# RWKV units: state decay and two products on GpSimd, the group norm's scaling and k's factor on ScalarE, one running sum per head pair

## The chip, the cores and the metric

The kernel runs on one core of a Trainium2 chip. The metric is the device time of one execution in microseconds. A core has five instruction queues that run beside each other, each in its own order, tied by semaphores: PE (TensorE, matmuls, with its weight loads listed as PEld), DVE (VectorE), ACT (ScalarE), POOL (GpSimd) and SP (SyncE, which here mostly issues DMA transfers).

## The reference

One layer of a hybrid decoder for a prompt of 1024 tokens and a group of 8 single tokens, in float32. One projection of the normalized input feeds three branches: RWKV-7 time mixing with 8 heads of 64, sliding-window attention, and cross-attention. They are merged with sigmoid gates, and a squared-ReLU MLP follows. The change lies in the RWKV branch alone:

```python
w_log = -softplus(-(w0 + tanh(wd) @ w2)) - 0.5
decay = exp(-exp(w_log));  a = sigmoid(a0 + ad @ a2);  g = sigmoid(gd) @ g2
kk = heads(k * k_k);  kk = kk / max(norm(kk), 1e-12)
kh = heads(k * (1 + (a - 1) * k_a))
# per head and token:
sa = S @ -kk_t
S  = S * decay_t + outer(sa, kk_t * a_t) + outer(v_t, kh_t)
y  = S @ r_t
# then a group norm over each head's 64 values:
y  = (y - mean(y)) * rsqrt(var(y) + 64e-5) * ln_w + ln_b
out = (y + sum(r * kh * r_k) * v) * g
```

## The kernel before

All 1032 tokens are held as columns, channels on partitions. A dense float32 product is made of three matmuls, since both sides are split into a high and a low part (`dense`, L181 to L183). `in_proj` (L254) makes 128 output columns of the input projection: 72 matmuls on weights of 512 KB; ScalarE casts the high part of the weights (L173), GpSimd subtracts it for the low part (L174).

The RWKV branch runs in chunks of 64 tokens. `unit(jj, q)` (L428) handles two pairs of heads and a quarter of the prompt, 256 tokens; a tile of 128 x 512 holds both pairs. There are eight units, the last of each jj with the 8 single tokens added. A unit is a generator in three parts:

- Preparation, to the first yield: loads of r, k, v (tiles zr, zk, zv); decay logarithm lw and a (tile aa) from two small products; running sums of lw within each chunk (L468); the norm of kk; k's factor (L490, L491); the products r·k (L494, L496) whose sums go through DRAM (`bsum`) and return spread over partitions as rn and bv; exponentials of the sums (L529, L530); and the two operands of the chunk products, BR (L533, L535) and CK (L534, L536).
- Inverse, to the second yield: GM = CK'BR, masked (L545, L548); its triangular blocks go through DRAM (`amat`) into AT, a tile of one buffer spread over all partitions (L574); a loop of 31 steps with two VectorE operations each (L581, L583) inverts them into X, which goes through DRAM (`xmat`) back into GM (L585, L588).
- Recurrence: XW and two block products (L590, L597, L600); four chunk steps, each with a product with the state (L616), two products with GM and the chunk's values (L619, L626) copied out by ScalarE (L622, L627), the state's increment (L629), the state update on VectorE (L631), and the output (L633, L635); then the group norm (L651 to L658), a transpose (L661), scaling (L665, L672) and the store.

What sets the order: the loop at L686 to L698 steps the units' generators against each other, unit u+1's preparation beside unit u's recurrence, with dense products (two pair projections, then gates, two of them at a time) as filler between. Within that, a scheduler lays out each engine's instructions by program order and its own estimated times; on the chip each engine takes them strictly in that order. `gates` stores its result through a ring of two buffers `gt` (L286, L287).

Of the kernel before, what the change touches and what calls it, by code (L numbers as in the profile page):

```python
# [13 lines left out]
ALU = mybir.AluOpType  # L14
# [4 lines left out]
P = 128  # L19
# [70 lines left out]
def tile_step(ctx, tc, I, O):  # L90
# [156 lines left out]
    def col(c):  # L247
        return pv[:, c:c + 1]
# [75 lines left out]
    SY.dma_start(g2, I["rw_g2"][0])  # L324
    hw0 = mk(rk, "hw0", [P, 12])
    V.tensor_scalar(hw0[:, 0:8], pv[:, C_W0:C_W0 + 8], 0.5, None, op0=ALU.mult)
    V.tensor_scalar(hw0[:, 8:12], pv[:, C_KA:C_KA + 4], -1.0, 1.0, op0=ALU.mult, op1=ALU.add)
    one64 = mk(rk, "one64", [P, CH])
    V.memset(one64, 1.0)
    bvs = mk(cp, "bvs", [P, 4, NS])  # L330
    gs = mk(cp, "gs", [P, 4, NS])
    states = [[mk(rk, f"st{j}{i}", [P, P]) for i in range(2)] for j in range(4)]
    for j in range(4):
        for i in range(2):
            G.memset(states[j][i], 0.0)
# [92 lines left out]
    def unit(jj, q):  # L428
# [32 lines left out]
        V.tensor_scalar(lw[:, :n], lw[:, :n], -HALF_E, -HALF_E, op0=ALU.mult, op1=ALU.add)  # L461
        V.tensor_scalar(aa[:, :n], aa[:, :n], 0.5, 0.5, op0=ALU.mult, op1=ALU.add)
        if end:
            sv = mk(ra, "sv", [P, 2, 6, NS])
            A.activation(sv[:, :, 1], lw[:, W:n].rearrange("p (j n) -> p j n", j=2), AF.Exp)
        for c in range(HN):
            cs = slice(c * CH, c * CH + CH)
            V.tensor_tensor_scan(lw[:, cs], one64, lw[:, cs], 0.0, ALU.mult, ALU.add)  # L468

# [17 lines left out]
        for e in range(2):  # L487
            i = 2 * jj + e
            for c in spans[e]:
                V.tensor_scalar(tmp[:, c], aa[:, c], col(C_KA + i), hw0[:, 8 + i:9 + i], op0=ALU.mult, op1=ALU.add)  # L490
        V.tensor_tensor(zk[:, :n], zk[:, :n], tmp[:, :n], ALU.mult)  # L491
# [18 lines left out]
        V.tensor_tensor(kk[:, :n], kk[:, :n], rn[:, :n], ALU.mult)  # L510
        V.tensor_tensor(bv[:, :n], bv[:, :n], zv[:, :n], ALU.mult)
        V.tensor_tensor(aa[:, :n], aa[:, :n], kk[:, :n], ALU.mult)
        if end:
            G.tensor_copy(bvs[:, pr], bv[:, W:n].rearrange("p (j n) -> p j n", j=2))
            for i, t in ((0, zr), (2, zk), (3, zv), (4, kk), (5, aa)):
                G.tensor_copy(sv[:, :, i], t[:, W:n].rearrange("p (j n) -> p j n", j=2))
            b = sm_bank([12 * NS, P])
            PE.transpose(b, sv.rearrange("p e a b -> p (e a b)"), ident)
            svt = mk(ra, "shr", [NS * NRT, P])[0:12 * NS]
            A.activation(svt, b, AF.Copy)  # L520
            for e in range(2):
                SY.dma_start(svec_d.rearrange("a b n -> (a b) n")[:, js[e]], svt[e * 6 * NS:(e + 1) * 6 * NS])
# [10 lines left out]
        V.scalar_tensor_tensor(BR[:, :, 0], ch(kk), -1.0, ex[:, :, 0:CH], ALU.mult, ALU.mult)  # L533
        V.tensor_tensor(CK[:, :, 0], ch(aa), ch(lw), ALU.mult)  # L534
        V.tensor_tensor(BR[:, :, 1], ch(zr), ex[:, :, 1:CH + 1], ALU.mult)  # L535
        V.tensor_tensor(CK[:, :, 1], ch(zk), ch(lw), ALU.mult)  # L536
# [38 lines left out]
        X = mk(rp, "X", [P, 8, 32])  # L575
        V.tensor_copy(X, xinit)
        for s in range(31):
# [32 lines left out]
        for cc in range(4):  # L610
            ST = [states[2 * jj + e] for e in range(2)]
            S, S2 = [t[cc % 2] for t in ST], [t[(cc + 1) % 2] for t in ST]
            cs = [cc, 4 + cc]
            pp = cp_bank([P, 2, P])
            for e in range(2):
                PE.matmul(pp[:, e], lhsT=BR[:, cs[e]].rearrange("p a t -> p (a t)"), rhs=S[e], start=e == 0, stop=True,  # L616
                          skip_group_check=e > 0)
            for e, hh, hs in both:
                PE.matmul(pp[0:64, e, hs], lhsT=GM[64:128, cs[e], hh, 0:64], rhs=UV[64:128, cs[e], hs], start=False,  # L619
                          stop=True, skip_group_check=True)  # L620
# [7 lines left out]
            for e, hh, hs in both:  # L628
                PE.matmul(ps[hs, e], lhsT=CKT[:, cs[e], hs], rhs=UV[:, cs[e], hs], start=True, stop=True)  # L629
            for e, hh, hs in both:  # L630
                V.scalar_tensor_tensor(S2[e][hs, hs], S[e][hs, hs], gc[hs, cs[e]:cs[e] + 1], ps[hs, e], ALU.mult, ALU.add)  # L631
            for e, hh, hs in both:
# [3 lines left out]
        if end:  # L636
            b = cp_bank([P, 2, P])
            for e in range(2):
                PE.transpose(b[:, e], states[2 * jj + e][0], ident)
            so = mk(rp, "so", [P, 2, 64])  # L640
# [9 lines left out]
        for i in range(8):  # L650
            V.bn_stats(st[:, i], Y[:, i // 2, (i % 2) * 64:(i % 2) * 64 + 64])  # L651
            V.bn_aggr(ag[:, i], st[:, i])
        vv = mk(rp, "gvv", [P, 3, 8])
        V.tensor_scalar(vv[:, 0], ag[:, :, 1], 64e-5, None, op0=ALU.add)
        rsqrt(vv[:, 0], vv[:, 1], vv[:, 2])
        for i in range(8):
            ys = Y[:, i // 2, (i % 2) * 64:(i % 2) * 64 + 64]
            V.tensor_scalar(ys, ys, ag[:, i, 0:1], vv[:, 1, i:i + 1], op0=ALU.subtract, op1=ALU.mult)  # L658
        b = cp_bank([P, 4, P])
# [1108 lines left out]
```

## Time and profile before

| | |
|---|---|
| median of three runs | 2059.64 us (2055.43, 2059.64, 2061.08) |
| profiled execution | 2062.78 us, span 2061.0 us, mean granted clock 0.948 |
| PE busy | 1928.9 us (94%) |
| VectorE busy | 1344.0 us (65%) |
| ScalarE busy | 755.8 us (37%) |
| GpSimd busy | 590.7 us (29%) |
| RWKV units | about 185 to 700 us of the span |

The profile is of one execution. "Busy" of an engine counts its instructions' time; a row of the waits says which instruction stood, and which work ended its wait. The granted clock is that of TensorE as a share of full speed: 0.50 is the lower of its two levels (1.2 GHz), 1.0 the upper (2.4 GHz). "xN" counts instructions; in a row of lines, the first number behind the bar is the total in us, the second the mean of one in ns.

### The profile page before, as it was taken

To read this page: it belongs to the slowest core of one execution; us is meant where nothing else is said; L and a number is where in the kernel's file an instruction comes from. 1 tells how busy PE (TensorE), PEld (TensorE's weight loads), DVE (VectorE), ACT (ScalarE), POOL (GpSimd) and SP (SyncE) were. 2 spreads that over 40 slices of the span, in tenths; PEclk is the share of its full clock that TensorE was granted. 3 is DMA by queue.
4 is the path that set the end of the run, shared out by engine and by line. 5 is a ranking of instruction groups with operands and counts; after the bars stand their busy time and mean duration, and the time that the engine had idled before them with its cause. 6 is when DMAs were issued, how large, how long until landed. Compare 5 with 4: busy or idle time off the path is not lost. (4 is left out here: it accounts for less than half of the span.)

```text
span 2061.0 us, 36994 instructions
## 1 busy us (share of the span) xinstructions
PE 1928.9 (94%) x14079; PEld 1834.5 (89%) x14079; DVE 1344.0 (65%) x3247; ACT 755.8 (37%) x1617; POOL 590.7 (29%) x606
## 2 busy tenths in 40 slices
PE   4989999998999989999989999979999998999998
PEld 4879888887888888989979999969999998999997
DVE  7465667576676457477652575687666669788864
ACT  4432323232322335344652123343333344344433
POOL 3422211111111135322020000146655554344421
PEclk9999788799898999999999999989999999999999
DMA  4544322323232145232236346416544448455413
GB/s 142 169 152 130 88 73 80 90 80 93 60 84 70 30 129 168 85 95 79 65 112 212 109 142 206 123 49 197 166 150 137 149 150 288 126 148 159 141 40 101
DMA packets 257104, 250.69 MB, mean 122 GB/s; under 512 B 43102, under 2 KB 204959, under 8 KB 256927
## 3 DMA queue, kind: packets, MB, share of 16 engines
q1 hardware_dynamic: 254656, 241.24, 38.5%
q0 software_dynamic: 2016, 6.53, 1.0%
q8 instruction: 111, 1.82, 0.4%
q14 instruction: 67, 0.54, 0.1%
q10 hardware_dynamic: 254, 0.55, 0.1%
HBM read 174.19 MB, written 74.46 MB: 121 GB/s over the span
## 5 line engine op out<-in xcount | busy, mean ns | idle before, releaser
L181 PE MATMUL mm<-hh,wh 128*128 128x384 f32 (+1 forms) x1152 | 391.7, 340 | 5.7 <-ACT z L342 5.1
L182 PE MATMUL mm<-hl,wh 128*128 128x384 f32 (+1 forms) x1152 | 390.0, 339 | 7.3 <-DVE hl L217 7.3
L183 PE MATMUL mm<-hh,wl 128*128 128x384 f32 (+1 forms) x1152 | 390.5, 339 | 1.3 <-POOL wl L174 1.3
L1555 PE MATMUL z<-h,wl 128*128 128x258 f32 x1488 | 265.6, 287 | 7.9 <-DVE x L1648 4.5
L1555 PE MATMUL z<-h,wh 128*128 128x258 f32 x1488 | 263.2, 285 | 8.1 <-DVE wh L1310 4.9
L182 PEld LDWEIGHTS mm<-hl,wh 128*128 128x128 f32 x1152 | 227.6, 198 | 11.3 <-DVE hl L217 8.2
L181 PEld LDWEIGHTS mm<-hh,wh 128*128 128x128 f32 x1152 | 228.5, 198 | 10.1 <-ACT z L342 5.6
L183 PEld LDWEIGHTS mm<-hh,wl 128*128 128x128 f32 x1152 | 228.3, 198 | 5.1 <-POOL wl L174 1.7
L1555 PEld LDWEIGHTS z<-h,wl 128*128 128x128 f32 x1488 | 217.6, 193 | 9.8 <-ACT wl L1536 5.0
L1555 PEld LDWEIGHTS z<-h,wh 128*128 128x128 f32 x1488 | 216.1, 192 | 9.2 <-DVE wh L1310 5.1
L174 POOL TENSOR_TENSOR wl<-wst,wh 128x1024 fp32r<-128x1024 f32 x48 | 116.9, 2435 | 215.6 <-ACT wh L173 211.1
L1648 DVE TENSOR_TENSOR x<-z,x 128x516 f32<-128x516 f32 x168 | 115.9, 691 | 68.8 <-PE z L1555 65.5
L1555 PE MATMUL z<-l,wl 128*128 128x258 f32 x744 | 154.7, 288 | 3.1 <-DVE l L1310 3.1
L1555 PE MATMUL z<-l,wh 128*128 128x258 f32 x744 | 153.5, 286 | 1.0 <-DVE l L1310 1.0
L173 ACT ACTIVATE wh<-wst 128x1024 fp32r<-128x1024 f32 x84 | 88.8, 1057 | 141.4 <-PE mm L182 75.0
L1555 PEld LDWEIGHTS z<-l,wl 128*128 128x128 f32 x744 | 117.9, 192 | 3.7 <-DVE l L1310 3.6
L1555 PEld LDWEIGHTS z<-l,wh 128*128 128x128 f32 x744 | 117.0, 191 | 1.7 <-DVE l L1310 1.7
L1503 POOL TENSOR_TENSOR sw<-wst 128x256 f32<-128x256 f32 (+1 forms) x56 | 55.1, 984 | 208.0 <-DMA wst<-in_w_down 87.9
L1607 POOL TENSOR_TENSOR us<-us,us 128x516 f32<-128x516 f32 x64 | 96.5, 1519 | 52.0 <-issue 22.1
L1310 DVE TENSOR_TENSOR l<-ub,h 128x516 fp32r<-128x516 f32 (+1 forms) x120 | 92.9, 800 | 6.3 <-ACT h L1335 6.1
L183 PE MATMUL mm<-oh,wl 128*128 128x384 f32 (+1 forms) x288 | 92.2, 320 | 0.0
L182 PE MATMUL mm<-ol,wh 128*128 128x384 f32 (+1 forms) x288 | 92.1, 320 | 0.0
(510 smaller groups left out, 4281.1 us busy)
## 6 DMA issues: line engine op xcount, KB each, us to landing
u<-us SPq DMA_DIRECT2D x112, 258.0 KB
ub<-u SPq DMA_DIRECT2D x112, 258.0 KB
wst<-in_w_in SPq DMA_DIRECT2D x48, 512.0 KB
wst<-in_w_down SPq DMA_DIRECT2D x24, 512.0 KB
gate<-gt SPq DMA_DIRECT2D x48, 192.0 KB
gl<-gate SPq DMA_DIRECT2D x16, 516.0 KB
wst<-in_w_out SPq DMA_DIRECT2D x16, 512.0 KB
wst<-in_w_up SPq DMA_DIRECT2D x16, 512.0 KB
```

The costliest lines, as they stand in the source:

```text
L173: A.activation(hi, st, AF.Copy)
L174: last_lo[:] = [eng.tensor_tensor(lo, st, hi.bitcast(F32), ALU.subtract)]
L181: PE.matmul(out, lhsT=wh, rhs=xh, start=first and k == 0, stop=False)
L182: PE.matmul(out, lhsT=wh, rhs=xl, start=False, stop=False)
L183: end = PE.matmul(out, lhsT=wl, rhs=xh, start=False, stop=last and k == n - 1)
L1310: V.tensor_tensor(lo, x, hi.bitcast(F32), ALU.subtract)
L1503: G.tensor_tensor(s[:, k:k + n], v, w, op)
L1555: op = PE.matmul(z[:, s, :HQ], lhsT=t[:, a, k], rhs=right[ks[k], s, i][b], start=go and k + q == 0, stop=q == 2 and k == nk - 1, skip_grou ...
L1607: G.tensor_tensor(t, x, y, ALU.subtract)
L1648: V.tensor_tensor(c, z, c, ALU.add)
```

## The change

The state of two head pairs lies in one tile. Its decay is computed by GpSimd ahead of time into a new tile dS (two instructions a chunk), and the update on VectorE becomes two sums over both pairs in place of four fused operations. Two products over the whole unit, bv times v (before L511) and BR's second half (before L535), move to GpSimd, and so does the copy into X (before L576). The scaling of the group norm (before L658, eight per unit) moves to ScalarE, with its bias computed by two small GpSimd operations from mean and reciprocal deviation. k's factor (before L490) moves to ScalarE; a is kept as tanh, so that L462 goes and the half is put into other constants. The eight running sums of 64 become two of 256 with a multiplier that is 0 at each chunk's start.

```diff
@@ -322,15 +322,18 @@
...
-    hw0 = mk(rk, "hw0", [P, 12])
+    hw0 = mk(rk, "hw0", [P, 16])
     V.tensor_scalar(hw0[:, 0:8], pv[:, C_W0:C_W0 + 8], 0.5, None, op0=ALU.mult)
-    V.tensor_scalar(hw0[:, 8:12], pv[:, C_KA:C_KA + 4], -1.0, 1.0, op0=ALU.mult, op1=ALU.add)
-    one64 = mk(rk, "one64", [P, CH])
-    V.memset(one64, 1.0)
+    V.tensor_scalar(hw0[:, 8:12], pv[:, C_KA:C_KA + 4], -0.5, 1.0, op0=ALU.mult, op1=ALU.add)
+    V.tensor_scalar(hw0[:, 12:16], pv[:, C_KA:C_KA + 4], 0.5, None, op0=ALU.mult)
+
+    carry = mk(rk, "carry", [P, 4, CH])
+    V.memset(carry, 1.0)
+    V.memset(carry[:, :, 0:1], 0.0)
     bvs = mk(cp, "bvs", [P, 4, NS])
     gs = mk(cp, "gs", [P, 4, NS])
-    states = [[mk(rk, f"st{j}{i}", [P, P]) for i in range(2)] for j in range(4)]
-    for j in range(4):
+    states = [[mk(rk, f"st{j}{i}", [P, 2, P]) for i in range(2)] for j in range(2)]
+    for j in range(2):
         for i in range(2):
             G.memset(states[j][i], 0.0)
@@ -459,13 +462,12 @@
...
         V.tensor_scalar(lw[:, :n], lw[:, :n], -HALF_E, -HALF_E, op0=ALU.mult, op1=ALU.add)
-        V.tensor_scalar(aa[:, :n], aa[:, :n], 0.5, 0.5, op0=ALU.mult, op1=ALU.add)
...
-        for c in range(HN):
-            cs = slice(c * CH, c * CH + CH)
-            V.tensor_tensor_scan(lw[:, cs], one64, lw[:, cs], 0.0, ALU.mult, ALU.add)
+        for e in range(2):
+            cs = slice(e * Q4, e * Q4 + Q4)
+            V.tensor_tensor_scan(lw[:, cs], carry.rearrange("p c t -> p (c t)"), lw[:, cs], 0.0, ALU.mult, ALU.add)
@@ -487,7 +489,7 @@
         for e in range(2):
             i = 2 * jj + e
             for c in spans[e]:
-                V.tensor_scalar(tmp[:, c], aa[:, c], col(C_KA + i), hw0[:, 8 + i:9 + i], op0=ALU.mult, op1=ALU.add)
+                A.activation(tmp[:, c], aa[:, c], AF.Identity, bias=hw0[:, 8 + i:9 + i], scale=hw0[:, 12 + i:13 + i])
         V.tensor_tensor(zk[:, :n], zk[:, :n], tmp[:, :n], ALU.mult)
@@ -508,12 +510,13 @@
...
         V.tensor_tensor(kk[:, :n], kk[:, :n], rn[:, :n], ALU.mult)
-        V.tensor_tensor(bv[:, :n], bv[:, :n], zv[:, :n], ALU.mult)
-        V.tensor_tensor(aa[:, :n], aa[:, :n], kk[:, :n], ALU.mult)
+        G.tensor_tensor(bv[:, :n], bv[:, :n], zv[:, :n], ALU.mult)
+        V.scalar_tensor_tensor(aa[:, :n], aa[:, :n], 1.0, kk[:, :n], ALU.add, ALU.mult)
         if end:
             G.tensor_copy(bvs[:, pr], bv[:, W:n].rearrange("p (j n) -> p j n", j=2))
-            for i, t in ((0, zr), (2, zk), (3, zv), (4, kk), (5, aa)):
+            for i, t in ((0, zr), (2, zk), (3, zv), (4, kk)):
                 G.tensor_copy(sv[:, :, i], t[:, W:n].rearrange("p (j n) -> p j n", j=2))
+            G.tensor_scalar(sv[:, :, 5], aa[:, W:n].rearrange("p (j n) -> p j n", j=2), 0.5, None, op0=ALU.mult)
@@ -531,8 +534,8 @@
         G.tensor_copy(gc, ex[:, :, CH])
         BR, CK = mk(rp, "BR", [P, HN, 2, CH], F32, 2), mk(ra, "CK", [P, HN, 2, CH])
         V.scalar_tensor_tensor(BR[:, :, 0], ch(kk), -1.0, ex[:, :, 0:CH], ALU.mult, ALU.mult)
-        V.tensor_tensor(CK[:, :, 0], ch(aa), ch(lw), ALU.mult)
-        V.tensor_tensor(BR[:, :, 1], ch(zr), ex[:, :, 1:CH + 1], ALU.mult)
+        G.tensor_tensor(BR[:, :, 1], ch(zr), ex[:, :, 1:CH + 1], ALU.mult)
+        V.scalar_tensor_tensor(CK[:, :, 0], ch(aa), 0.5, ch(lw), ALU.mult, ALU.mult)
         V.tensor_tensor(CK[:, :, 1], ch(zk), ch(lw), ALU.mult)
@@ -573,7 +576,7 @@
...
         X = mk(rp, "X", [P, 8, 32])
-        V.tensor_copy(X, xinit)
+        G.tensor_copy(X, xinit)
@@ -608,13 +611,18 @@
...
         for cc in range(4):
-            ST = [states[2 * jj + e] for e in range(2)]
-            S, S2 = [t[cc % 2] for t in ST], [t[(cc + 1) % 2] for t in ST]
+            S, S2 = states[jj][cc % 2], states[jj][(cc + 1) % 2]
             cs = [cc, 4 + cc]
             pp = cp_bank([P, 2, P])
             for e in range(2):
-                PE.matmul(pp[:, e], lhsT=BR[:, cs[e]].rearrange("p a t -> p (a t)"), rhs=S[e], start=e == 0, stop=True,
+                PE.matmul(pp[:, e], lhsT=BR[:, cs[e]].rearrange("p a t -> p (a t)"), rhs=S[:, e], start=e == 0, stop=True,
                           skip_group_check=e > 0)
+
+            dS = mk(rp, "dS", [P, 2, CH])
+            for hh in range(2):
+                hs = slice(hh * 64, hh * 64 + 64)
+                G.tensor_tensor(dS[hs], S[hs, :, hs], gc.rearrange("p (e c) -> p e c", e=2)[hs, :, cc:cc + 1].to_broadcast([64, 2, CH]),
+                                ALU.mult)
             for e, hh, hs in both:
@@ -627,8 +635,9 @@
...
-            for e, hh, hs in both:
-                V.scalar_tensor_tensor(S2[e][hs, hs], S[e][hs, hs], gc[hs, cs[e]:cs[e] + 1], ps[hs, e], ALU.mult, ALU.add)
+            for hh in range(2):
+                hs = slice(hh * 64, hh * 64 + 64)
+                V.tensor_tensor(S2[hs, :, hs], dS[hs], ps[hs], ALU.add)
@@ -650,12 +659,14 @@
...
-        vv = mk(rp, "gvv", [P, 3, 8])
+        vv = mk(rp, "gvv", [P, 4, 8])
         V.tensor_scalar(vv[:, 0], ag[:, :, 1], 64e-5, None, op0=ALU.add)
         rsqrt(vv[:, 0], vv[:, 1], vv[:, 2])
+        G.tensor_tensor(vv[:, 3], ag[:, :, 0], vv[:, 1], ALU.mult)
+        G.tensor_scalar(vv[:, 3], vv[:, 3], -1.0, None, op0=ALU.mult)
         for i in range(8):
             ys = Y[:, i // 2, (i % 2) * 64:(i % 2) * 64 + 64]
-            V.tensor_scalar(ys, ys, ag[:, i, 0:1], vv[:, 1, i:i + 1], op0=ALU.subtract, op1=ALU.mult)
+            A.activation(ys, ys, AF.Identity, bias=vv[:, 3, i:i + 1], scale=vv[:, 1, i:i + 1])
```

The scheduler lays out the queues anew. On VectorE, before: the rows that lead up to the first read of unit 6's AT (L581 with AT_5533). Names with sn, tmp, zr, zk belong to unit 7's preparation.

```order
L126 SCALAR_TENSOR_TENSOR sn_5877<-sn_5877 128x10
L491 TENSOR_TENSOR zk_5811<-zk_5811,tmp_5862 128x528
L127 SCALAR_TENSOR_TENSOR sn_5877<-sn_5877 128x10
L494 SCALAR_TENSOR_TENSOR tmp_5862<-zr_5810,pv_74_422,zk_5811 128x256
L125 TENSOR_TENSOR sn_5877<-sn_5877 128x10
L494 SCALAR_TENSOR_TENSOR tmp_5862<-zr_5810,pv_74_422,zk_5811 128x8
L126 SCALAR_TENSOR_TENSOR sn_5877<-sn_5877 128x10
L494 SCALAR_TENSOR_TENSOR tmp_5862<-zr_5810,pv_74_422,zk_5811 128x256
L581 TENSOR_TENSOR xt_5537<-X_5535,AT_5533 128x31
L127 SCALAR_TENSOR_TENSOR sn_5877<-sn_5877 128x10
```

After, the same place: GM_5462 and AT_5514 are unit 6's, XW_4897 and the state sums (st from dS and cp) unit 5's.

```order
L551 TENSOR_TENSOR GM_5462<-sm_5464,gmask_574 128x4x128
L593 STREAM_TRANSPOSE XW_4897<-GM_4847 32x512
L551 TENSOR_TENSOR GM_5462<-sm_5475,gmask_574 128x4x128
L551 TENSOR_TENSOR GM_5462<-sm_5476,gmask_574 128x4x128
L575 STREAM_TRANSPOSE XW_5512<-GM_5462 32x512
L640 TENSOR_TENSOR st_128_602<-dS_5293,cp_5302 64x2x64 x2
L640 TENSOR_TENSOR st_127_601<-dS_5322,cp_5331 64x2x64 x2
L584 TENSOR_TENSOR xt_5518<-X_5516,AT_5514 128x31
L586 TENSOR_TENSOR X_5516<-X_5516,xt_5518 128x31
```

Before, unit 7's k factor, its r·k products and the steps of its norm stood ahead of the first read, and ahead of these the group norm's scaling and the running sums; the last product L548 of unit 6 lay 39 rows further up. After, three rows lie between the last product (L551) and the first read (L584).

On GpSimd, before, where units 2 and 3 are worked on (wl is the low part of filler weights):

```order
L174 TENSOR_TENSOR wl_3205<-wst_3202,wh_3204 128x1024
L339 MEMSET z_3108 128x1
L344 COPY zl_567<-z_3108 128x9
L174 TENSOR_TENSOR wl_3773<-wst_3770,wh_3772 128x1024
L339 MEMSET z_3200 128x1
L531 COPY gc_2661<-tmp_2612 128x8
L556 TENSOR_TENSOR CK_2667<-CK_2667,gc_2661 128x512
L516 COPY sv_3332<-zr_3291 128x2x8
L556 TENSOR_TENSOR CK_2667<-CK_2667,gc_2661 128x512
```

After, with the same filler weights' first one (wl_3757 was wl_3773) at the top; dS is the state's decay, gvv the group norm's small vectors:

```order
L174 TENSOR_TENSOR wl_3757<-wst_3754,wh_3756 128x1024
L342 MEMSET z_3185 128x1
L665 TENSOR_TENSOR gvv_2378<-gag_2361,gvv_2378 128x8
L666 TENSOR_SCALAR gvv_2378<-gvv_2378 128x8
L624 TENSOR_TENSOR dS_2711<-st_126_600,gc_1929 64x128 x2
L513 TENSOR_TENSOR bv_2632<-bv_2632,zv_2567 128x512
L624 TENSOR_TENSOR dS_2740<-st_125_599,gc_1929 64x128 x2
L347 COPY zl_567<-z_3185 128x9
L174 TENSOR_TENSOR wl_3847<-wst_3844,wh_3846 128x1024
```

Where there were weight parts, small copies and the product of CK with gc, the state decays now stand between them: dS_2711 behind a weight part and two norm operations, dS_2740 behind bv's product, which itself waits for bv's transfer.

## Rows read from the trace of the kernel before

**Rows 1.** The page's busy time of each engine with its share of the span and its instructions, and the granted clock of PE in 40 equal slices of the span, in tenths.

```profile
PE 1928.9 (94%) x14079; PEld 1834.5 (89%) x14079; DVE 1344.0 (65%) x3247; ACT 755.8 (37%) x1617; POOL 590.7 (29%) x606
...
PEclk9999788799898999999999999989999999999999
```

**Rows 2.** The stretch of the RWKV units: its length, busy us (and instructions) of PE, PEld, DVE, ACT and POOL, PE's granted clock, DMA's share, GB/s.

```profile
185.00:700.00 515.00, 482.85 (x3453) 426.60 (x3452) 342.32 (x1324) 155.72 (x348) 75.42 (x94) 0.88 0.29 80
```

**Rows 3.** What PE waited for in 185 to 700 us: the waiting instruction's line, what ended the wait, us in total, times, longest.

```profile
PE sm L496 <- DVE tmp L494: 9.6, 4, 5.1
PE sm L545 <- DVE CK L534: 5.1, 2, 2.8
PE cp L597 <- DMA GM<-xmat: 4.1, 1, 4.1
PE cp L597 <- DVE X L583: 3.6, 1, 3.6
PE sm L545 <- DVE GM L548: 2.5, 4, 0.7
PE cp L661 <- DVE Y L658: 2.0, 1, 2.0
PE sm L545 <- DVE BR L535: 1.9, 2, 1.3
...
PE cp L616 <- DVE st L631: 0.6, 1, 0.6
```

**Rows 4.** Stretches with the clock at 0.50, columns as in rows 2. A stall of PE at L545 came just before the first three, one at L496 before the last two.

```profile
206.40:213.20 6.80, 6.80 (x42) 6.29 (x39) 3.28 (x5) 1.62 (x4) 2.08 (x2) 0.50 0.10 18
...
244.00:254.20 10.20, 10.20 (x48) 9.09 (x49) 8.06 (x19) 0.62 (x2) 2.61 (x3) 0.50 0.35 108
...
363.40:373.70 10.30, 10.30 (x48) 9.32 (x48) 8.21 (x43) 2.48 (x6) 2.39 (x3) 0.50 0.27 74
...
397.60:418.00 20.40, 20.40 (x114) 17.93 (x114) 11.00 (x42) 4.64 (x11) 0.25 (x3) 0.50 0.23 65
510.20:534.10 23.90, 21.51 (x118) 19.14 (x119) 13.58 (x53) 5.13 (x12) 0.25 (x3) 0.50 0.24 67
```

**Rows 5.** VectorE's groups of instructions by line and shape in 185 to 700 us: count, total us, mean ns, and the idle time before them.

```profile
L631 DVE SCALAR_TENSOR_TENSOR st<-st,gc,cp 64x64 f32<-64x64 f32 x128 | 35.9, 280 | 48.6 <-PE cp L629 30.4 <-ACT UV L627 11.8 <-ACT gt L286 4.1
...
L658 DVE TENSOR_SCALAR Y<-Y,gag,gvv 128x64 f32<-128x64 f32 x64 | 15.0, 309 | 0.1
L468 DVE TENSOR_TENSOR_SCAN lw<-one,lw 128x64 f32<-128x64 f32 x56 | 12.0, 272 | 0.0
...
L494 DVE SCALAR_TENSOR_TENSOR tmp<-zr,pv,zk 128x256 f32<-128x256 f32 x16 | 7.7, 482 | 0.0
...
L511 DVE TENSOR_TENSOR bv<-bv,zv 128x512 f32<-128x512 f32 x6 | 6.2, 1039 | 0.0
L490 DVE TENSOR_SCALAR tmp<-aa,pv,hw 128x256 f32<-128x256 f32 x15 | 6.0, 404 | 0.0
...
L535 DVE TENSOR_TENSOR BR<-zr,tmp 128x512 f32<-128x512 f32 x8 | 5.5, 685 | 0.0
```

**Rows 6.** GpSimd's groups of the same view.

```profile
L174 POOL TENSOR_TENSOR wl<-wst,wh 128x1024 fp32r<-128x1024 f32 x20 | 49.0, 2448 | 145.1 <-ACT wh L173 145.1
L556 POOL TENSOR_TENSOR CK<-CK,gc 128x512 f32<-128x512 f32 x16 | 17.3, 1078 | 28.9 <-PE sm L545 28.7
```

**Rows 7.** ScalarE's groups of the same view.

```profile
L475 ACT ACTIVATE kk<-zk,pv 128x256 f32<-128x256 f32 x14 | 6.7, 498 | 1.3 <-DVE BR L533 1.3
...
L503 ACT ACTIVATE shr<-sm 20x128 f32<-20x128 f32 x8 | 2.1, 263 | 5.3 <-PE sm L501 5.3
```

**Rows 8.** VectorE in order of time from 388 us: start, duration in us, instruction, and in brackets the idle time before it with what ended it.

```profile
389.42 0.42 DVE L462 TENSOR_SCALAR aa<-aa 128x512 f32<-128x512 f32 x1
389.75 0.29 DVE L576 COPY X<-xinit 128x256 f32<-128x256 f32 x1
...
395.27 0.19 DVE L581 TENSOR_TENSOR xt<-X,AT 128x31 f32<-128x31 f32 x1 [3.36 <-DMA AT<-amat]
```

**Rows 9.** PE in order of time, just behind that.

```profile
397.27 0.78 PE L496 MATMUL sm<-c_hsel,tmp 128*128 128x2 f32 x4 [2.41 <-DVE tmp L494]
```

**Rows 10.** VectorE in order of time at another first read of AT.

```profile
510.58 0.19 DVE L581 TENSOR_TENSOR xt<-X,AT 128x31 f32<-128x31 f32 x1 [4.38 <-DMA AT<-amat]
```

**Rows 11.** SP in order of time: the issue of the transfer that this read waited for.

```profile
496.75 2.62 SPq L574 DMA_DIRECT2D AT<-amat  x1
```

**Rows 12.** GpSimd and VectorE in order of time around 359 us.

```profile
358.86 2.47 POOL L174 TENSOR_TENSOR wl<-wst,wh 128x1024 fp32r<-128x1024 f32 x1 [3.15 <-ACT wh L173]
...
359.01 2.40 DVE L583 TENSOR_TENSOR X<-X,xt 128x64 f32<-128x64 f32 x1
...
362.19 0.24 DVE L583 TENSOR_TENSOR X<-X,xt 128x75 f32<-128x75 f32 x1
```

**Rows 13.** Waits of VectorE, ScalarE and GpSimd in 185 to 700 us, columns as in rows 3.

```profile
DVE st L631 <- PE cp L629: 30.4, 20, 3.2
DVE xt L581 <- DMA AT<-amat: 15.4, 3, 7.7
...
ACT gt L286 <- DMA gate<-gt: 30.4, 4, 11.5
...
POOL wl L174 <- ACT wh L173: 145.1, 19, 20.6
```

More of the change, by code (lines that the diff above doesn't have):

```diff
@@ L638, in unit @@
             for e in range(2):
-                PE.transpose(b[:, e], states[2 * jj + e][0], ident)
+                PE.transpose(b[:, e], states[jj][0][:, e], ident)
             so = mk(rp, "so", [P, 2, 64])
```

## Prediction

> **What bounds the kernel now.** I began with the page's busy times and clock digits [rows 1]. PE is busy for 94% of the span, so the whole is set by PE's work, its stalls and its clock; of the clock digits that stand below 9, all but one lie in the fifth to thirteenth of the 40 slices. The table by stretches [rows 2] puts numbers to it: in 185 to 700 us, where the eight RWKV units run, PE is busy for 482.9 of 515 us at a mean granted clock of 0.88. PE's list of matmuls is the same before and after, so in this stretch there are two things to win: the 515 − 482.9 = 32 us in which PE stands, and the time at half clock.
>
> The list of what PE waited for [rows 3] comes next. Of its sum I separate two kinds by looking at what VectorE itself had been doing. The stall of 5.1 us at L496 and that of 2.4 us at L496 [rows 9] come behind a VectorE that stood waiting for the AT load: at 395.27 for 3.36 us [rows 8], at 510.58 for 4.38 us [rows 10], with L490, L491 and L494 of the next unit queued behind it. L597's 4.1 us is a DMA outright, and its 3.6 us stall comes behind the longest AT wait, 7.7 us [rows 13]. These make 5.1 + 2.4 + 4.1 + 3.6 = 15.2 us that end with a transfer. What is left ends with VectorE's own work: L545 for CK 5.1, for GM 2.5, for BR 1.9, L661 for Y 2.0 and the rest of L496, 9.6 − 5.1 − 2.4 = 2.1: together 13.6 us. PE waited for a new state at L616 only once, 0.6 us.
>
> The last view is the table of the stretches in which the granted clock was 0.50, that is the lower level of 1.2 GHz [rows 4]. Three of those shown follow a stall that VectorE's work ended: 6.8 + 10.2 + 10.3 = 27.3 us. Two follow a stall behind the AT load: 20.4 and 23.9 us. Work at half clock takes twice as long, so half of each is loss: 13.7 us behind VectorE's own work, 22 us behind AT.
>
> **The change part by part, per unit (eight units).** VectorE loses:
> - L462, 0.42 us, and the copy of X at L576, 0.29 [rows 8].
> - Six of eight running sums. Eight at 272 ns [rows 5] make 2.18 us; two of 256 elements are not in the trace. If they cost by the element they save nothing; if like the 256-element L490 (404 ns) 1.37. I take 0.7, the middle.
> - L490, 2 × 0.404 = 0.81; L511 and L535, 0.69 each (L535's row; L511's 1.04 has a collision in it, below) [rows 5].
> - The state update: sixteen L631 of 280 ns are 4.48 us. Eight sums of twice the width replace them, between 280 ns and the 482 ns of a 256-element L494 [rows 5]; I take 320, nearer to L631, as they also read PSUM: 2.56, a gain of 1.9 (0.6 to 2.2).
> - The group norm's scaling, 8 × 309 ns = 2.47 [rows 5].
>
> Sum: 0.42 + 0.29 + 0.7 + 0.81 + 1.38 + 1.9 + 2.47 = 8.0 us a unit, 64 us in all, of 342 us that VectorE is busy in the stretch [rows 2].
>
> GpSimd gains bv and BR's second half, two products of 128x512 like L556, 1078 ns each [rows 6] (below that their 0.69 on VectorE, above it half of L174's 2448 ns for twice the width: 1.22); eight decays of 64x128 between a quarter of L556, 0.27, and all of it, 1.08: I take 0.35, nearer to the size; the X copy and two tiny ones. That is 2.16 + 2.8 = 5 us of two-operand work a unit, 40 us in all (36 to 86), beside 75 us that GpSimd is busy now. It fits into the idle time; what it does to VectorE is the question. The trace shows one collision plainly [rows 12]: while GpSimd's L174 ran for 2.47 us from 358.86, an L583 of VectorE that started at 359.01 took 2.40 us; the next L583 took 0.24. So the two engines exclude each other in such a pair. The price lies between nothing and all 40 us. VectorE is busy for 66% of the stretch, and I assume half of that to have two SBUF operands (the L581 and L583 of the loop, the products over a whole unit), so a third of the new GpSimd time meets it: 13 us, which is my value. VectorE's net gain is then about 51 us.
>
> The Trainium skill's "GPSIMD Engine Reference" (Key points) states the rule in general: GpSimd shares its SBUF interfaces with VectorE and contends with VectorE instructions that have two SBUF inputs. It speaks against this change. The collision above agrees with it; taken at its fullest, every new GpSimd product would be paid back on VectorE, 40 us, and 24 us of relief would remain.
>
> ScalarE gains two L490-like operations of about 498 ns and eight of 64 elements, between L503's 263 ns (128 columns, 20 partitions) and L475's 498 [rows 7]; I take 270: 1.0 + 2.2 = 3.2 us a unit, 25 us beside 156 us busy in 515: idle time hides it. For the group norm the path becomes VectorE, GpSimd twice, ScalarE, PE; I put 0.5 to 1.5 us on it. PE waited for this chain for 2.0 us in all, so a unit's norm mostly has slack and I cost it at nothing; without that cover it would be 8 × 1 = 8 us. It has one risk of its own: on ScalarE, L286 stood for 30.4 us in four waits until the gate buffer was free [rows 13], and what is queued behind it, now the norm too, stands with it.
>
> The state update on the path becomes shorter by two L631, 0.56 us a chunk, 18 us over 32 chunks. PE has dense matmuls between the steps and waited for states for just 0.6 us, so I take nothing from it; if it were the chain that paces the units, all 18 would come. VectorE itself stood 30.4 us at L631 for PE [rows 13]; that stays.
>
> **The sum.** Of the 13.6 us of stalls ended by VectorE's work, the front parts of a unit lose 2.9 us (L462, sums, L490, X, L511) ahead of L545, but BR's half now comes from a GpSimd that may stand behind L174 (145.1 us of waits for its cast [rows 13]), and PE's filler is placed anew. Between nothing and all 13.6, I take half: −7. Of the 13.7 us of clock loss behind them half as well: −7. The DMA-ended stalls stay: no transfer is made shorter. −14 us from the profiled run, 2062.78 (a span of 2061.0 and 1.8 around it), gives 2049; that run lies 3.1 us above the median of 2059.64, so for a median I predict 2046.
>
> **Rivals.**
> *The transfers pace the units (no change).* Each unit goes through three round trips to DRAM, and AT has one buffer. What VectorE gains it waits away at the next landing, or gives back to GpSimd in collisions (at the full 40 us). For it: more of PE's stall time, 15.2 of 32 us, and more clock loss, 22 us, stand behind DMA than behind VectorE. Against it: 13.6 us are VectorE's own, in rows that name CK, BR and GM. Time: 2060, within 6 us.
>
> *The AT load loses its cover (slower).* AT was issued at 496.75 [rows 11] and first used at 510.58, 13.8 us later; nothing in the change shortens that. What covers it is VectorE's other work between GM's last product and the loop's first read of AT. In the order of before, unit 6 has 39 instructions' rows there, the norm's scaling, the running sums, L490 and L511 among them; after the change three, a transpose and two rows of state sums. Where the cover is below 13.8 us VectorE stands, and the next unit's L494 and the state sums with it, then PE. Such an episode has a price in the trace: 5.1 us of stall and half of 23.9 us at half clock, 17 us. Before there are three AT waits [rows 13]; with two more, 34 − 14 = 20 us more: 2080. It decides from one more episode on (17 against 14). Against it: the two state sums wait for PE's steps, a chunk lasts some us, and that is cover of another kind.
>
> **How the numbers follow.** My forecast (faster) 0.48; no change 0.24; slower by lost cover 0.28. A measurement of this kernel can tell about 0.3%, 6 us, from no change, so these three are also the chances of faster, same and slower. The forecast's own range goes from 2014 (all of 13.6 + 13.7, and the 18 us of the state chain: −45) to 2053. The 8-in-10 range keeps 2014 and goes up to 2084, past the 2080 of two episodes; a third (2097) is left out.
>
> **What would show it right or wrong.** Right: in 185 to 700 VectorE's busy time falls by 45 to 60 us, PE's waits at L545 for CK, BR and GM fall by half, the granted clock of the stretch rises from 0.88 to about 0.90, and the units end some 14 us earlier. The second rival shows as more than three AT waits or more than 15.4 us of them, with L496 or L597 waiting behind; the first as unchanged PE waits with more idle time on VectorE. GpSimd at L556's price is right if bv and BR take 1.0 to 1.2 us; collisions show as L581 and L583 far above 0.25 us. If the state sums wait for decays (GpSimd named as their releaser) or the norm's scaling for a gate buffer, an edit that I costed at nothing costs. The prediction is wrong if the time is above 2053, and its mechanism is wrong too if it is below that while PE's waits at L545 are as they were.

## The result and the profile after

The changed kernel is slower: 2072.0 us (median of four runs, 2070.2 to 2074.2) against 2057.5 us, a ratio of 1.0071 with a 95% interval of 1.0048 to 1.0094. A later set gave 1.0052 (1.0019 to 1.0085). So it costs 10 to 15 us where 14 us of gain were forecast.

The page of the changed kernel, busy times and clock digits, against [rows 1]:

```profile
span 2068.2 us, 36968 instructions
...
PE 1928.9 (93%) x14079; PEld 1835.2 (89%) x14079; DVE 1305.7 (63%) x3021; ACT 786.1 (38%) x1701; POOL 643.8 (31%) x706
...
PEclk9999888989999999989989999979999999999999
```

VectorE did get its relief, 1344.0 − 1305.7 = 38 us; ScalarE took 30 us more, GpSimd 53. PE's busy time is the same. To compare stages I cut each run where PE has reached the same place in its list, the 630th and the 4400th matmul: between them lies all the work of the units and their filler. The stretches of the kernel before, from its first profile and from a second one, columns as in [rows 2]:

```profile
148.90:713.40 564.50, 532.32 (x3771) 476.07 (x3772) 362.60 (x1344) 168.90 (x372) 90.06 (x109) 0.89 0.29 82
713.40:925.00 211.60, 194.78 (x1302) 186.11 (x1301) 128.71 (x289) 86.17 (x203) 75.34 (x71) 0.97 0.40 118
```

```profile
147.80:704.60 556.80, 523.22 (x3771) 467.72 (x3772) 358.82 (x1344) 169.13 (x372) 89.46 (x109) 0.90 0.29 83
704.60:912.20 207.60, 192.47 (x1302) 183.34 (x1301) 127.36 (x289) 86.08 (x203) 75.35 (x71) 0.98 0.40 120
```

The same work in the changed kernel, again from two profiles:

```profile
148.50:708.50 560.00, 519.42 (x3771) 465.29 (x3772) 318.86 (x1123) 199.31 (x457) 145.70 (x213) 0.90 0.29 83
708.50:925.20 216.70, 197.31 (x1303) 187.86 (x1302) 131.43 (x289) 86.64 (x205) 74.92 (x71) 0.96 0.39 116
```

```profile
149.40:711.20 561.80, 523.40 (x3771) 469.23 (x3772) 319.14 (x1123) 198.95 (x456) 146.84 (x213) 0.89 0.29 82
711.20:925.10 213.90, 194.28 (x1303) 184.53 (x1301) 132.05 (x288) 86.27 (x203) 75.27 (x71) 0.98 0.39 117
```

The units last 561 us in the mean in both kernels, although VectorE is busy for 42 us less. PE's idle time (length minus PE busy) rose from 33 to 39.5 us; the clock of this stretch is the same in these profiles. The next stretch, in which both kernels run the same instructions in the same order, is 5.7 us longer, and what follows 3.3 us; these two make most of the difference of the profiles (2054.9 against 2064.7 us, means of two spans). With the half-clock loss (1 minus clock, times length) taken off as well, the units keep 460 to 470 us in both: PE's own work.

Two profiles are few, but every run lists its span and its mean granted clock, so the half-clock loss of the whole span can be had from all of them; what remains of the span is its work and stalls (a stall that falls into half clock counts half in each). In the later set the kernel before loses 101 us with a rest of 1958 (mean of 19 runs; ten more give 100 and 1956), the changed kernel 111 and 1957 (ten runs), and in the first set 115 and 1955 (four). These means are good to 2 or 3 us. So the rest did not move, and the 10 to 14 us that the change costs are time at half clock.

Which waits replaced which shows in what PE waited for in 185 to 700 us of the changed kernel, against [rows 3]:

```profile
PE sm L548 <- DVE GM L551: 11.0, 2, 7.7
PE cp L618 <- DVE st L640: 6.3, 4, 4.3
PE cp L600 <- DMA GM<-xmat: 5.5, 1, 5.5
PE cp L672 <- ACT Y L669: 4.3, 4, 1.8
PE sm L548 <- DVE CK L538: 3.6, 2, 3.3
PE sm L498 <- DVE tmp L496: 3.1, 3, 1.9
```

The wait for CK fell from 5.1 to 3.6, that for the r·k products from 9.6 (PE's L496 before) to 3.1 (L498 now), and the waits for BR and X (1.9, 3.6) are all but gone. In their place PE waits for the drained product GM (2.5 before, now 11.0), for states (0.6, now 6.3) and for the group norm (2.0, now 4.3). The largest, in order of time, on PE and then on VectorE and GpSimd of the changed kernel:

```profile
238.17 2.05 PE L548 MATMUL sm<-BR,CK 64*128 64x128 f32 x24
247.92 2.07 PE L548 MATMUL sm<-BR,CK 64*128 64x128 f32 x8 [7.71 <-DVE GM L551]
```

```profile
240.12 2.41 DVE L584 TENSOR_TENSOR xt<-X,AT 128x76 f32<-128x76 f32 x1
...
247.18 0.68 DVE L551 TENSOR_TENSOR GM<-sm,gmask 128x512 f32<-128x512 f32 x1
```

```profile
240.09 2.34 POOL L174 TENSOR_TENSOR wl<-wst,wh 128x1024 fp32r<-128x1024 f32 x1 [0.72 <-DVE X L586]
```

And the same products before:

```profile
243.88 3.74 PE L545 MATMUL sm<-BR,CK 64*128 64x128 f32 x24 [2.82 <-DVE CK L534]
...
249.77 2.07 PE L545 MATMUL sm<-BR,CK 64*128 64x128 f32 x8
```

```profile
247.64 0.68 DVE L548 TENSOR_TENSOR GM<-sm,gmask 128x512 f32<-128x512 f32 x1
```

PE came to the product 5.7 us earlier, and the first drain came 0.5 us earlier, since it stands in VectorE's queue behind the loop of the unit before, whose steps wait for each other (and one of which, at 240.12, took 2.41 us beside GpSimd's weight part of 240.09). PE's list changed as well: before, six dense matmuls stood between the first 24 products and the last 8, and the drain ended under them; now the last 8 follow at once, and PE stands for 7.71 us. What was won ahead of the product was stood out behind it. No run put the drain ahead of the loop, so how much of this wait is the loop and how much the moved filler is not shown.

What the new operations cost, in VectorE's, GpSimd's and ScalarE's groups (185 to 700 us):

```profile
L640 DVE TENSOR_TENSOR st<-dS,cp 64x128 f32<-64x128 f32 x64 | 18.3, 285 | 62.2 <-PE cp L637 56.9 <-ACT gt L286 4.2
...
L470 DVE TENSOR_TENSOR_SCAN lw<-carry,lw 128x256 f32<-128x256 f32 x14 | 9.9, 710 | 0.0
```

```profile
L624 POOL TENSOR_TENSOR dS<-st,gc 64x128 f32<-64x128 f32 x64 | 26.9, 420 | 153.2 <-DVE st L640 150.7
...
L537 POOL TENSOR_TENSOR BR<-zr,tmp 128x512 f32<-128x512 f32 x8 | 10.1, 1262 | 0.1
```

```profile
L669 ACT ACTIVATE Y<-Y,gvv 128x64 f32<-128x64 f32 x64 | 22.1, 427 | 11.6 <-POOL gvv L666 6.0 <-DVE xsn L127 3.4 <-DVE xt L584 2.1
```

The state sum took 285 ns (320 taken), a decay 420 (350), BR's half 1262 (1078), a norm scaling on ScalarE 427 (270), each against the value taken in the prediction. VectorE's own waits, against [rows 13]:

```profile
DVE st L640 <- PE cp L637: 56.9, 26, 4.2
DVE xt L584 <- DMA AT<-amat: 27.4, 5, 13.1
```

It stands 56.9 us at the state sum for PE (30.4 before) and 27.4 us for AT (15.4): what it saved, it mostly waits.

### The profile page after: what moved, and what is told of

It reads as the page before. It is cut to its first block, busy times and chain, and to the rows that moved or that the text cites. A ratio compares the mean times of both kernels' runs of the same rounds, so it can differ in the third digit from the quotient of the medians.

```text
span 2068.2 us, 36968 instructions
## 1 busy us (share of the span) xinstructions
PE 1928.9 (93%) x14079; PEld 1835.2 (89%) x14079; DVE 1305.7 (63%) x3021; ACT 786.1 (38%) x1701; POOL 643.8 (31%) x706
## 5 line engine op out<-in xcount | busy, mean ns | idle before, releaser
L183 PE MATMUL mm<-hh,wl 128*128 128x384 f32 (+1 forms) x1152 | 384.8, 334 | 1.4 <-POOL wl L174 1.4
```

The source lines that it names most:

```text
L183: end = PE.matmul(out, lhsT=wl, rhs=xh, start=False, stop=last and k == n - 1)
```

## The experiments

All ratios are to the kernel before, of the same set, with their 95% intervals. Stretch, PE's idle time and clock are those of the units, cut as above.

**Second profiles.** Both kernels, unchanged.

> The kernel before, unchanged, for a second profile. Both profiles so far agree to 0.2 us at the 5700th matmul (925 us) and the changed kernel's loses 7 us behind it, in stages that the change does not touch, with a lower clock there. Theory 'clock behind the units': those 7 us are chance of one execution, so this profile will have another sum of clock loss behind 925 us than the 28 us of the first one, by some us either way. Theory 'units': the first profile is typical, the units' stretch (630th to 4400th matmul) lasts 564 us within 3, with 32 us of PE stalls. Time 2054 to 2061 by both.

> The changed kernel, unchanged, for a second profile. Theory 'units': its first profile was lucky in the units' stretch (560 us although PE's stalls there are 8 us more than before, 40.6 against 32.2); the second one has 570 to 575 us there, and the loss of 14 us lies in the stalls. Theory 'clock behind the units': the stretch again lasts about 560 us and the loss lies again behind 925 us, 7 us or more, at a lower clock. Time 2070 to 2074 by both.

Before: 0.9977 (0.9950 to 1.0005). Changed: 1.0052. The rows are above. Both theories missed half: the changed kernel's stretch is not longer than before, and what it lost behind 925 us in the first profile was not there in the second (1136.0 us, as before). So single spans of either kernel move by some 10 us, and the units' gain does not exist.

**The change in parts.** Each part alone on the kernel before, and all parts without the decay. The edits are the hunks of the change; in this order, their core: running sums; group norm; k factor (with a kept as tanh); products (BR's half and X's copy likewise); decay.

```diff
-        for c in range(HN):
+        for e in range(2):
...
-            V.tensor_scalar(ys, ys, ag[:, i, 0:1], vv[:, 1, i:i + 1], op0=ALU.subtract, op1=ALU.mult)
+            A.activation(ys, ys, AF.Identity, bias=vv[:, 3, i:i + 1], scale=vv[:, 1, i:i + 1])
...
-                V.tensor_scalar(tmp[:, c], aa[:, c], ...)
+                A.activation(tmp[:, c], aa[:, c], AF.Identity, ...)
...
-        V.tensor_tensor(bv[:, :n], bv[:, :n], zv[:, :n], ALU.mult)
+        G.tensor_tensor(bv[:, :n], bv[:, :n], zv[:, :n], ALU.mult)
...
+                G.tensor_tensor(dS[hs], S[hs, :, hs], ...)
+                V.tensor_tensor(S2[hs, :, hs], dS[hs], ps[hs], ALU.add)
```

> Only the running sums: two of 256 in place of eight of 64, nothing moves to another engine. Theory 'own price': it takes about 0.7 us of VectorE a unit, 6 us in all, so the time is 2054 to 2061, the median of before (2060 in the last job) or a little less. Theory 'order': what counts is where the scheduler puts VectorE's loop, AT's first read and the products GM against PE's list when any time in its estimate moves; then even this edit moves the time by 10 us or more, either way, with stalls of PE at other places than before.

> Only the group norm's scaling moved to ScalarE, with two small GpSimd operations. Own price: VectorE gets 2.47 us a unit, 20 us in all, back; the chain from rsqrt to PE grows by 1 us a unit: 2052 to 2064. Order: 10 us or more from 2060, either way.

> Only k's factor moved to ScalarE, with a kept as tanh: VectorE loses 1.2 us a unit, 10 us in all. Own price: 2054 to 2062. Order: 10 us or more from 2060, either way.

> Only bv, BR's second half and the copy into X moved to GpSimd. Own price: VectorE gets 1.7 us a unit back, 13 us in all, and GpSimd's products return about a third of their 2.2 us a unit in collisions: 2054 to 2064. If a copy or product that stands in GpSimd's queue behind a transfer is what harms (X at 276.9 us stood 11 us there in the changed kernel), 2066 to 2075 with that wait in the trace. Order: 10 us or more from 2060, either way, without such a wait on the way of a stall.

> Only the state's decay moved to GpSimd, with the paired states. If the decay is the harmful part (state sums now need GpSimd, which stands in its queue behind weight parts, and the filler is placed anew), 2066 to 2072. If it is not, its shorter update gives 2050 to 2060.

> All of the change but the state's decay. If the decay is the harmful part, 2045 to 2060. If the harm is in the other parts or in the lost cover of the AT load (first reads of AT move up because VectorE has less to do), it stays: 2066 to 2076.

| kernel | ratio | stretch, us | PE idle, us | clock |
|---|---|---|---|---|
| running sums | 1.0089 (1.0050 to 1.0129) | 588.2 | 38.1 | 0.85 |
| group norm | 0.9987 (0.9959 to 1.0015) | 562.5 | 35.0 | 0.89 |
| k factor | 1.0072 (1.0036 to 1.0108) | 573.1 | 45.0 | 0.90 |
| products, X | 1.0173 (1.0121 to 1.0225) | 593.8 | 54.7 | 0.88 |
| decay | 1.0115 (1.0047 to 1.0182) | 585.0 | 42.7 | 0.87 |
| all but decay | 1.0158 (1.0102 to 1.0213) | 596.4 | 50.7 | 0.86 |

No part gains, and they do not add up: the decay costs 1.2% alone, the rest 1.6%, both together 0.5 to 0.7%. Both decay runs came out above either range given for them. "Own price" holds for the group norm only. The running sums are the plainest: two of 684 ns replace eight of 272, less work asked of the same engine, and the time rises. VectorE's busy time in the stretch does not even fall (367.0 us, against 362.6 and 358.8), since the loop's operations take 124.6 us there in place of 114.6. Its loss is clock: 0.15 of 588 us is 88 us, against 56 and 62 in the two profiles of before. In one place, the stretches of that kernel, columns as in [rows 2]:

```profile
326.80:334.80 8.00, 8.00 (x66) 6.26 (x66) 5.16 (x8) 4.29 (x11) 2.71 (x2) 1.00 0.47 139
334.80:348.40 13.60, 13.60 (x72) 12.00 (x71) 7.50 (x35) 2.47 (x9) 0.20 (x1) 0.50 0.22 60
```

PE shows no idle time there, but its list held small products of two units (16 of L602, 4 of L618, 28 more of 64 columns, and the preparation's L458 and L459, down to 8 columns) with one dense matmul among them; then the clock fell to 0.50 for 13.6 us. My prediction had priced such stretches only behind stalls.

**A redrawn order without a change.** One copy into a tile that nobody reads, per unit, in the kernel before (64 columns) and in the changed one (16):

```diff
+        dead = mk(ra, "dead", [P, 64])
+        V.tensor_copy(dead, lw[:, 0:64])
         kk, tmp = mk(ra, "kk", [P, WS]), mk(ra, "tmp", [P, WS])
```

> The kernel before with one copy of 128x64 per unit on VectorE into a tile that nobody reads: eight copies of some 0.15 us, about 1 us of work in all. Theory 'own price': 2058 to 2064, the time before within 2 us. Theory 'order': the scheduler's order of all engines differs from the 896th PE row on, as it did with the running sums alone; the time moves by 10 us or more, and as with those mostly through TensorE at half clock in the units' stretch (85 us of loss there with the sums alone, 53 and 63 before), with PE's stalls within 6 us of the 33 of before.

> The changed kernel with one copy of 128x16 per unit on VectorE into a tile that nobody reads, about 1 us in all. If the scheduler's order is a lottery with steps of 10 to 20 us, it is 5 us or more from the changed kernel's 2070, either way, with stalls at other places. If the changed kernel's time is a property of what was moved, within 4 us of it.

Before with the copy: 1.0011 (0.9980 to 1.0043), stretch 559.0 us. Changed with the copy: 1.0114 (1.0065 to 1.0164), 572.0 us. So "any new order moves the time by 10 us" fell for the kernel before, whose PE list departs from the old one at 225 us, at no cost; the changed kernel moved by some 0.5%, though the two intervals touch. A new order can cost, as the running sums suggest, but need not.

**Single suspects of the changed kernel.** X's copy back on VectorE (ScalarE's list is the same, PE's nearly so); bv's product, BR's half and X's copy all back; and the loop held behind the state sums:

```diff
-        G.tensor_copy(X, xinit)
+        V.tensor_copy(X, xinit)
...
+                for op in (list(last_st.values()) if s == 0 else ()):
+                    behind.enter_context(tc.issue_after(op.ins))
```

> The changed kernel with the copy into X back on VectorE; the order of PE, ScalarE and SP stays as it was almost to the row. VectorE's wait of 11.2 us for GpSimd's copy at the first read of unit 1's AT goes, or becomes the wait of the copy itself for the transfer of X as before (6.4 us); PE's stall at L600 falls from 5.4 to the 4.1 of before. If a copy in GpSimd's queue is what harms: 2050 to 2060. If it only stands where PE has filler: within 4 us of the changed kernel's 2069 to 2072.

> The changed kernel with bv, BR's second half and X back on VectorE: GpSimd keeps the state's decay and the norm's small operations. If collisions of these products with VectorE's loop are what made the 7.7 us stall at L548 for GM and the rest (own price): 2050 to 2062, that stall under 4 us. If the order decides: 10 us or more from the changed kernel's 2070, either way.

> The changed kernel, with the loop's first operation of each unit put behind the last state sum of the unit before, so that no state sum stands behind a wait for AT. Theory 'lost cover': the stalls at L618 for st (6.3 and 6.4 us in the two profiles) go to under 1 us, VectorE's waits for AT fall below 10 us, and the time falls to 2050 to 2062. Rival: the loop starts later, and the units' end moves back by more than that; 2070 to 2090. Order redrawn: anything, with the stalls at L618 gone.

X: 1.0035 (0.9998 to 1.0073), within noise of the changed kernel; VectorE's one wait of 11.2 us for that copy was not what cost. Products back: 1.0068 (1.0029 to 1.0106), and the stall for GM still 6.5 us at 246 us: not the products' doing. The guard: 1.0623 (1.0543 to 1.0703), far above both of its ranges. PE's waits for states and VectorE's for AT are gone, but over the stretch, now 696 us, PE waits 46.6 us for xmat and 25.6 us behind XW instead. State sums behind a wait for AT do cost (4.30 us at 629.67 in the changed kernel, behind VectorE's 6.93 at 626.63), but far less than giving up the overlap.

**Without AT's transfer.** AT loaded for the first unit only, in both kernels; the other seven loops compute on its values.

```diff
+        if not once:
+            once.append(mk(ra, "AT", [P, NT])[:, :1024].rearrange("p (s t) -> p s t", t=32))
+            SY.dma_start(once[0], ...)
+        AT = once[0]
```

> The kernel before, with AT loaded for the first unit alone and reused by the other seven, so that their loops compute on another unit's blocks and wait for no AT. Theory 'lost cover': before had little to lose by AT, about one episode of 17 us; 2040 to 2060. Theory 'transfers pace the units': the round trip is part of what sets the units' stretch, the 15 us of PE stalls that end with a transfer and the 22 us of clock loss behind them go: 2020 to 2045.

> The changed kernel with AT loaded once in the same way. Theory 'lost cover': with the AT waits gone (27 us of VectorE's waits) the relief of VectorE shows, and this kernel is 10 to 20 us faster than the one before without AT's loads. Theory 'relief is worth nothing, the order decides': it is not faster than that one by more than 5 us, and may be slower.

Before: 0.9835 (0.9776 to 0.9895). Changed: 0.9954 (0.9919 to 0.9990). First the kernel before, then the changed one:

```profile
148.90:683.80 534.90, 513.82 (x3771) 462.33 (x3772) 363.84 (x1344) 168.71 (x373) 93.08 (x109) 0.92 0.28 80
```

```profile
147.70:695.20 547.50, 520.67 (x3770) 468.37 (x3771) 319.56 (x1123) 198.88 (x456) 145.61 (x213) 0.90 0.27 78
```

By the ratio AT's transfer is worth 34 us in the kernel before; 26 us of it show in the units of this profile, 12 as stalls of PE and the rest by the clock. Without it the changed kernel is still behind, by 1.2% and by 12.6 us in this stretch. Over all runs that is clock alone: with AT left out half clock costs 78 us in the kernel before (four runs, rest 1947) and 103 us in the changed one (ten runs, rest 1946). So its AT waits are not what hid the gain. The 7.7 us stall for GM is there still.

**The moved work left out.** The changed kernel without the decay, bv times v, the norm's scaling and k's factor (none of these is computed).

> The changed kernel with most of the moved work left out altogether: no decay of the state, no product of bv with v, no scaling of the group norm, no k factor; BR's second half and X's copy stay on GpSimd. VectorE has the changed kernel's list, GpSimd and ScalarE are relieved of some 45 and 30 us. If collisions on SBUF and the queues of GpSimd and ScalarE took the gain, this is 15 us or more faster than the kernel before: 2030 to 2048. If VectorE's relief is worth little because PE waits for other things, 2052 to 2070.

1.0020 (0.9985 to 1.0054).

```profile
150.80:714.90 564.10, 521.61 (x3771) 468.61 (x3772) 316.36 (x1123) 168.88 (x372) 103.91 (x125) 0.90 0.29 82
```

```profile
PE cp L613 <- DVE st L630: 8.1, 4, 4.6
PE sm L543 <- DVE GM L546: 7.2, 3, 6.2
PE cp L595 <- DMA GM<-xmat: 5.8, 1, 5.8
```

This is the experiment that decides most. VectorE has the relief, GpSimd keeps little of the burden (BR's half and X's copy; in the units it is busy for 104 us, against 146 in the changed kernel and 90 before), ScalarE none, and in the order that this edit gets the kernel is as fast as before. The largest waits are again those of the changed kernel. What was left out costs the 0.3 to 0.5% between this and the changed kernel, with what the new order adds or takes.

**AT in pieces.** The kernel before, with AT's transfer in two pieces of 8 and 24 rows, and in four.

```diff
-        SY.dma_start(AT, a_d[u]....to_broadcast([4, 32, 32, 32]))
+        for s0, s1 in zip((0, 8), (8, 32)):
+            SY.dma_start(AT[:, s0:s1], a_d[u, :, :, s0:s1]....to_broadcast([4, 32, s1 - s0, 32]))
```

> The kernel before with AT loaded in four pieces of 4, 6, 8 and 14 of its 32 rows in place of one transfer, so that the loop can start when the first 64 KB have landed. If the wait is for the transfer's length, VectorE's waits for AT (15 us in three) fall below 6 us and the time by 5 to 15 us of the 31 that leaving AT out gave: 2045 to 2055 against 2060. If it is for the fixed way through DRAM, or the more issues on SP's queue hold up other transfers, 2058 to 2070.

> The kernel before with AT in two pieces of 8 and 24 rows, one issue more per unit. If the wait is for the transfer's length, 2048 to 2057, the waits for AT below 9 us; if for the fixed way, 2057 to 2065.

Four: 0.9956 (0.9925 to 0.9986). Two: 0.9857 (0.9833 to 0.9882), 2029.3 us, faster than both kernels and below both of its ranges. An issue and a first read that stood until the first of two pieces had landed:

```profile
529.71 0.57 SPq L575 DMA_DIRECT2D AT<-amat  x1
```

```profile
534.34 0.19 DVE L582 TENSOR_TENSOR xt<-X,AT 128x31 f32<-128x31 f32 x1 [3.20 <-DMA AT<-amat]
```

The same for a whole transfer, in the changed kernel:

```profile
321.95 0.56 SPq L577 DMA_DIRECT2D AT<-amat  x1
```

```profile
331.33 0.19 DVE L584 TENSOR_TENSOR xt<-X,AT 128x31 f32<-128x31 f32 x1 [4.11 <-DMA AT<-amat]
```

The stretch with two pieces:

```profile
149.90:683.60 533.70, 503.03 (x3770) 450.15 (x3771) 366.52 (x1344) 168.59 (x373) 90.78 (x109) 0.95 0.31 87
```

The first piece was read 4.6 us after its issue, the whole transfer 9.4 us. (The 13.8 us of [rows 10, 11] hold an issue that itself took 2.62 us on SP; all three transfers that the kernel before waits for have such an issue.) PE's idle time is 30.7 us, near that of before; the clock is 0.95, and the gain is there: over all runs half clock costs 72 us in place of 103, with a rest of 1956 in both. Both versions cut the waits for AT (four pieces to 0.2 us, two to 5.6 us), yet two pieces gain three times as much. How much of it is the shorter wait and how much the redrawn order was not separated.

## Why the prediction was wrong

- **What bounds the kernel**: right in kind. The units are PE's work plus stalls plus half clock, and the part laid to transfers (15.2 us of stalls, of which 4.1 at xmat, and 22 us of clock loss) was confirmed for AT: taking its transfer out gave 12 us of stalls in the units, and over all runs 24 us of half-clock loss.
- **VectorE's relief**: 38 us by the page, where 51 were worked out. The state sum was sized right (18 us gained where 15 were taken); the running sums gave about 2 us (12.0 to 9.9), where 5.6 were taken. What VectorE lost again elsewhere is more than the 13 us taken: the loop's operations took 129.0 us against 114.6, the first product of kk 8.8 against 5.5, BR's first half 7.6 against 5.5, together 20 us. That is not the price of the added GpSimd work alone: the loop took 124.6 us with the running sums alone, which give GpSimd nothing, and 132.7 with most of the added work left out. It meets GpSimd's old weight parts more often, as at 240.12. Such pairs agree with the Trainium skill's "GPSIMD Engine Reference" (Key points), contention with VectorE instructions that have two SBUF inputs, though not at its fullest (40 us). It did not decide the time: without most of that GpSimd work the kernel is no faster than before.
- **The step that failed is the sum's first term**: "Between nothing and all 13.6, I take half: −7". I treated these stalls as if only the operations ahead of them counted. At the largest of them the preparation did get shorter, PE did arrive earlier, and VectorE's next operation for PE stood behind the previous unit's loop. PE's idle time in the units went from 33 to 39.5 us, and over all runs work and stalls together did not fall. The second term, −7 us of clock loss behind them, failed with it and in its sign: the half-clock loss rose by 10 to 14 us. The first failure accounts for the missing gain, the second for the kernel being slower.
- **Half clock** was priced only behind stalls. In one place it followed a run of small products without a stall, which suggests that the place of the filler counts; with the running sums alone, the clock of the units was 0.85.
- **The first rival** (transfers pace the units, no change) is nearest for the units: 561 us before and after, the relief spent in waits. But the transfer that it names is not the reason; without it the relief shows no more.
- **The second rival** (lost cover) was right in its signs: VectorE's AT waits rose from three (15.4 us) to five (27.4 us), and state sums stood behind one. As the cause of the loss it fell with the runs without AT, where the changed kernel stays 1.2% behind; that its 2080 lies near the measured 2072 is luck. Its 13.8 us of needed cover were too many: the five waited reads of the changed kernel come 9 to 11 us after their issues.
- **Open**: why TensorE runs longer at half clock in the changed kernel. Over all runs that is the whole loss, but the two profiles do not place it: in their means it lies behind the units (5.7 and 3.3 us), in stretches that run the same instructions in the same order, and among the other kernels the first of these lasts 206 to 219 us. Nor was it tried to give the changed kernel the order of before.

## What to carry to other kernels

A less busy engine gains only what the operation that PE waits for next lets through: look up in the queue what stands behind the shortened part, and if it is a chain of dependent steps, count nothing. Before work is moved, leave it out for one run; if that gains nothing, moving it will hardly gain. Where a scheduler lays out the queues, measure one neutral edit too, since a new order can cost as much as the edit was meant to bring. And split every run's time into half-clock loss and rest before explaining it: here the rest of both kernels is the same.

## What the runs showed that I had not expected

- Two running sums of 256 elements took 684 ns each where eight of 64 took 272 each: cheaper per element, and the kernel 0.9% slower, nearly all of it at half clock (123 us lost against 105).
- Of a transfer of 512 KB in two pieces, the reader could start on the first 4.6 us after its issue, where the whole took 9.4; that kernel ran 1.4% faster, all of it by less time at half clock.
- ScalarE's scaling of 64 columns with scale and bias from tiles took 427 ns in the mean, beyond the 378 ns of its 256-column copies.
